# Query projection of a macaron block as a Strassen group, and first sums of weight pairs made by early adding transfers

## The chip, the cores and the metric

The kernel runs on one core of a Trainium2 chip. The metric is the device time of one execution in microseconds (us). The kernel before was timed three times. The engines are named as in the profile: PE (TensorE, matmuls), PEld (its weight loads), DVE (VectorE), ACT (ScalarE), POOL (GpSimd) and SP (SyncE); SP, ACT and POOL also issue transfers (DMAs).

## The reference

One encoder block on 256 frames of width 2048, in float32:

```python
x = x + 0.5 * swiglu_ffn(rmsnorm(x, g1), w_gate1, w_up1, w_down1)      # width 5632
h = rmsnorm(x, gm)
q_a, k_a, v_a, q_r, k_r, v_r, g_r, gate_a, gate_r = split(h @ w_in)    # 7 x 1024, 2 x 2048 columns
branch_a = chunked_band_attention(q_a, k_a, v_a, rel_bias) @ w_out_att # 8 heads of 128
branch_r = (silu(g_r) * retention(rotary(q_r), rotary(k_r), v_r)) @ w_out_ret
x = x + (sigmoid(gate_a) * branch_a + sigmoid(gate_r) * branch_r) @ w_out
x = x + 0.5 * swiglu_ffn(rmsnorm(x, g2), w_gate2, w_up2, w_down2)
return rmsnorm(x, gf)
```

Nearly all the work is matrix products of 256 rows with weights that are read once from HBM.

## The kernel before, in words

**Products in three parts.** Operands are split into a high part of reduced precision and the rest: ACT casts the high half (L129, tile hi), DVE subtracts it (L130, tile lo). A product takes three matmuls (L140, L141, L143): activation high with weight high, activation low with weight high, activation high with weight low. Matmuls run with 128x128 stationary activations and 512 weight columns.

**Plain steps.** A `Gemm` is a weight block of 512 columns; its K dimension is walked in steps of 256 rows. One step needs one weight transfer of 512 KB (raw, on SP's queue, five buffers), one split (one ACT and one DVE operation of 128x1024) and 2 x 2 x 3 = 12 matmuls. A job with K = 2048 has 8 steps.

**Strassen groups.** Two weight blocks of 512 columns that multiply the same activations are taken together as a 2x2 block product (rows halves by K halves) with 7 instead of 8 block products. A group has 28 steps of 6 matmuls: three phases of 8 (four r steps and four s steps, one for each of four pairs jc of row slices) and a last phase of four s steps. For each pair, two weight tiles k and x (512 KB each) come by POOL's queue (L543). The first sum x + k is formed either by DVE (`first`, L532) when the pair's r step is prepared, or by a transfer that adds in place (L547) for the pairs in `added`. In the second phase DVE adds a loaded weight to x (L594) and forms x - k (L580), and POOL issues a further adding transfer (L581). POOL's queue is strictly in order. The FFNs pass `ADDED`; the mixers' groups passed nothing, so there DVE formed all four first sums.

**Order.** All steps of the program stand in one list. `weave` lays it out: `lead` plain steps first, then the groups, with plain steps put between pairs of group steps. After each pair, a credit grows by rate x share of that place (`SHARE`, `MIX_SHARE`); from 0.6 on (0.2 at the end of a phase), and always at the end of the third phase, one plain step follows. A down projection's step may come only when `at_hand` says that its input is ready. `run` walks the list: before step c, up to four later steps are prepared (splits); then functions that are due at c (`later`, `at`) are called; then its matmuls are issued. Each engine executes in this program order, so a late DVE operation delays all DVE operations behind it. Loads of groups are released by `room["kept"]`: 8 transfers ahead, and `extra` more where `weave` is told so (the FFNs).

**Stages.** First FFN (10 groups, block 10 plain: a gate job and an up job; then down jobs), mixers (7 plain jobs and 5 groups woven, `mixed` is the step after), one more plain job, the retention's query and key jobs with attention and retention between them, output projections, second FFN. In the first FFN the plain gate job starts before the norm's scale is known: its results wait in two banks of tag z until `GATE_WAIT` steps later Silu is applied (L748), while the squares for the norm are summed by ACT (L429) in steps 8 to 11, two per step. `att_qk_done`, `nat_done` scale a projection; `to_transposed` transposes it on PE. Attention heads start at `mixed` + 4, one every four steps; q, k and v stay in SBUF from their projection until then (the pool of act tiles has 30 buffers).

Of the kernel before, what the change touches and what calls it, by code (L numbers as in the profile page):

```python
# [8 lines left out]
F32 = mybir.dt.float32  # L9
# [6 lines left out]
P = 128  # L16
# [24 lines left out]
MIX_LEAD = 8  # L41
RET_WAIT = (14, 5)
HELD = 6

MIX_SHARE = (0.85,) * 4 + (1.0,) * 4 + (0.8,) + (0.4,) * 3 + (0.15,) * 4
SHARE = (0.75,) * 4 + (1.0,) * 4 + (0.0,) * 4 + (0.2,) * 4
ADDED = (2, 3)
PLAIN = 10
PASSES = ((10,),) + tuple((b,) for b in range(10))
GATE_WAIT = 5  # L50
WARM = (6, 3)
TAIL_PARTS = ((0, slice(0, NB)), (1, slice(0, NB // 2)), (1, slice(NB // 2, NB)))

# [22 lines left out]
def block_kernel(ctx: ExitStack, tc: tile.TileContext, x, g1, w1g, w1u, w1d, gm, w_in, rel, woa, wor, wo,  # L76
# [439 lines left out]
    class Strassen:  # L516
# [2 lines left out]


        def __init__(self, norm, w1, col1, w2, col2, evict, added=()):
            self.added = added
# [15 lines left out]
        def loads(self):  # L538


            def go(tiles, i, jc):
                tiles[jc] = apool.tile([P, KC, NB], F32, tag="act", name=f"{self.name}{'kx'[i]}{jc}")
                nc.gpsimd.dma_start(tiles[jc], chunk(self.w[i], self.rows(0, jc), self.col[i]))  # L543

            def add_on():
                for jc in self.added:
                    nc.gpsimd.dma_start(self.x[jc], chunk(self.w[0], self.rows(0, jc), self.col[0]), accum_op=ALU.add)  # L547

            out = [
                lambda tiles=tiles, i=i, jc=jc: go(tiles, i, jc)  # L550
                for jc in range(HALF_K // KC) for i, tiles in enumerate((self.kept, self.x))
            ]
            out[-1] = lambda last=out[-1]: [last(), add_on()]
            return out

        def steps(self):

# [9 lines left out]
        def step(self, phase, jc, of_sum):  # L567
            made = {}
            name = f"{self.name}{phase}{jc}{'rs'[of_sum]}"
            n = HALF_K // KC  # L570

            def load():
                made["raw"] = weights_tile(f"raw{name}")
                i = 2 - phase
                fetch(made["raw"], self.w[i], self.rows(1, jc), self.col[i])

            def third():

                x, k = self.x[jc], self.kept[jc]
                nc.vector.tensor_sub(k, x, k)  # L580
                nc.gpsimd.dma_start(x, chunk(self.w[0], self.rows(1, jc), self.col[0]), accum_op=ALU.add)  # L581

            def prep():
                x = self.x[jc]
                if not of_sum:
                    if phase == 0:
                        made["w"] = split(self.kept[jc], name)
                        if jc not in self.added:
                            self.first(jc)
                        return  # L590
# [12 lines left out]

            bank, form, fresh, closing = {
# [4 lines left out]
            }[phase, of_sum]  # L609

            def products():
                hi, lo = made["w"]
                if fresh and jc == 0:
                    self.bank(bank)
                three([
                    (
                        self.acc[bank], self.norm.form(form, KC * jc + i), (hi[:, i, :], lo[:, i, :]),
                        fresh and jc == 0 and i == 0, closing and jc == n - 1 and i == KC - 1,
                    )
                    for i in range(KC)  # L620
                ], True)
# [59 lines left out]
    def weave(jobs, apart, groups, lead, share, start=None, extra=0):  # L681
# [5 lines left out]
        def next_standard():  # L687

            if len(queue) <= apart:
                return False  # L690
            job, k = queue[0]
            if any(at_hand.get(b, len(steps) + 1) > len(steps) for b in job.needs):
                return False
            steps.append(standard(job, k))
            del queue[0]
            if job.makes is not None and k + KC == job.nk:
                at_hand[job.makes] = len(steps) + 6
            return True

        for _ in range(lead):  # L700
# [27 lines left out]
    def ffn(name, norm, wg, wu, wd, after, start=None):  # L728
# [10 lines left out]
        def plain(b):  # L739
            gates = {}  # L740

            wait = GATE_WAIT if start is not None and b == PLAIN else 0

            def gate_done(acc):
                def go():
                    for t in range(NT):
                        gates[t] = tmp_tile(f"{name}g{b}{t}", "gate", 2)
                        nc.scalar.activation(gates[t], acc[t], AF.Silu, scale=norm.scale(t))  # L748

                if wait:  # L750
                    later(wait, go)
                else:
                    go()

            def up_done(acc):
                for t in range(NT):
                    a = gates[t]
                    nc.vector.scalar_tensor_tensor(a, acc[t], norm.scale(t), a, op0=ALU.mult, op1=ALU.mult)  # L758
                later(4, lambda: put_mid(b, gates))

            tags = ("acc", "acc")
            up = Gemm(wu, 0, b * NB, D // P, norm, up_done, tags)
            up.makes = b
            return [Gemm(wg, 0, b * NB, D // P, norm, gate_done, ("z", "z") if wait else tags), up]

        def paired(b):
            got = {}
# [59 lines left out]
    QA, KA, VA, QR, KR, VR, GR, GA, GG = 0, W, 2 * W, 3 * W, 4 * W, 5 * W, 6 * W, 7 * W, 7 * W + D  # L827
    scale = HD ** -0.5
    tposed, nat = {}, {}

    def heads_t(ts):
        return slice(ts * P, (ts + 1) * P)

    def to_transposed(key, b, srcs, steps):

        dst = act_tile(F32, f"{key}{b}T")
        tposed[key, b] = dst

        def go(t):
            ps = transpose4(srcs[t], f"{key}{b}p{t}").rearrange("p (i q) -> p i q", i=4)  # L840
# [4 lines left out]

        for t in range(NT):
            later(steps[t], lambda t=t: go(t))

    def att_qk_done(key, b):
        def done(acc):  # L850
# [40 lines left out]
    def nat_done(key, b, func, after=None):  # L891
        def done(acc):
            dst = act_tile(F32, f"{key}{b}")
            nat[key, b] = dst.rearrange("p a q -> p (a q)").rearrange("p (t n) -> p t n", t=NT)
            for t in range(NT):
                nc.scalar.activation(nat[key, b][:, t, :], acc[t], func, scale=nm.scale(t))
            if after is not None:
                after()

        return done  # L900
# [63 lines left out]
    def all_attention():  # L964
        for h in range(HEADS):
            for s, stage in attention(h):
                later(2 + 4 * h + s, stage)

    def retention(b):

# [65 lines left out]
    def gates(col1, col2, func, dsts):  # L1036
# [235 lines left out]
```

## Time and profile before

| | |
|---|---|
| median of three runs | 2061.91 us (2061.66 to 2061.99) |
| the profiled execution, its time | 2061.97 us |
| its span in the profile | 2060.1 us |
| PE, DVE, ACT, POOL busy | 2037.8, 1766.2, 1494.1, 344.8 us |
| matmuls | 9208 |
| moved by transfers | 498.47 MB, mean 242 GB/s |
| granted TensorE clock | 0.998 |

All durations below come from the one profiled execution. Its time and its span differ by 1.9 us of start and end around the program. A line of the costliest groups or of the timeline names line, engine, operation, out<-in by the program's tile names (buffer numbers left out); in the timeline, start and duration stand first, and in brackets the engine's idle time before it with what ended it. A group's tiles are named by the step at which the group stands: in z118, hiz11801s is the high half of phase 0, pair 1, s step. In rows of stages: start:end length, then busy us and instructions for PE, PEld, DVE, ACT, POOL; granted clock; share of the 16 DMA engines; GB/s.

### The profile page before, as it was taken

The page shows a single profiled execution, that of the slowest core. Times are in us where ns is not written, and L with a number is a line of the kernel's source. Part 1 is how long each engine was busy: PE and PEld are TensorE (multiplying, and loading weights), DVE is VectorE, ACT ScalarE, POOL GpSimd, SP SyncE. Part 2 cuts the span into 40 slices and gives each one's busy share as a digit, 9 for nine tenths or more (in the row PEclk, how much of TensorE's full clock was granted, in tenths as well). Part 3 has the DMA queues.
Part 4 walks back from the last instruction along what each step waited for, and adds up shares of the span by engine and source line. Part 5 has one row for each costly group of instructions (what it writes and reads, how often), then busy time and mean ns, then how long its engine had stood idle before and what let it go on. Part 6 is the DMA issues. An engine that isn't in the chain of part 4 may idle for free.

```text
span 2060.1 us, 26318 instructions
## 1 busy us (share of the span) xinstructions
PE 2037.8 (99%) x9208; PEld 1685.6 (82%) x9208; DVE 1766.2 (86%) x1836; ACT 1494.1 (73%) x1892; POOL 344.8 (17%) x386
## 2 busy tenths in 40 slices
PE   9999999999999999999999999999999999999998
PEld 7888888888888888888888888888888888888886
DVE  7999999999999799889966667569989999989996
ACT  8778877887877767776765434556788888887875
POOL 2221222221222110121100000012122212112200
PEclk9999999999999999999999999999999999999999
DMA  9888899888888677898786645578889888889983
GB/s 308 252 232 260 252 274 273 254 229 252 254 250 244 241 206 262 263 288 240 228 277 184 216 142 189 185 231 218 267 267 278 255 255 234 269 261 268 276 214 133
DMA packets 230325, 498.47 MB, mean 242 GB/s; under 512 B 15584, under 2 KB 16336, under 8 KB 230192
## 3 DMA queue, kind: packets, MB, share of 16 engines
q1 hardware_dynamic: 156736, 301.50, 43.5%
q0 software_dynamic: 70112, 189.44, 36.0%
q10 hardware_dynamic: 3344, 5.84, 0.8%
q8 instruction: 72, 1.18, 0.2%
q14 instruction: 61, 0.50, 0.1%
HBM read 487.81 MB, written 8.91 MB: 241 GB/s over the span
## 4 chain that ended last, share of the span: by engine, by line
PE 92%; ACT 3%; DVE 3%; issue 1%; DMA 1%; DVEq 0%; ACTq 0%; POOLq 0%; POOL 0%
PE acc L143 15%; PE acc L140 15%; PE acc L141 15%; DVE lo L130 1%; DMA raw<-in_w_in_dram 1%; ACT hi L129 0%; PE z392a L143 0%; PE z873a L140 0%; PE z910a L141 0%; PE z765a L141 0%; PE z543a L143 0%; PE z430a L143 0%; PE z801a L143 0%; PE z392a L141 0%; PE z505a L143 0%
## 5 line engine op out<-in xcount | busy, mean ns | idle before, releaser
L130 DVE TENSOR_TENSOR lo<-raw,hi 128x1024 fp32r<-128x1024 f32 x367 | 447.1, 1221 | 142.6 <-ACT hi L129 140.8
L129 ACT CAST hi<-raw 128x1024 fp32r<-128x1024 f32 x367 | 384.3, 1051 | 173.3 <-PE acc L141 138.0
L794 ACT ACTIVATE xall<-acc 128x512 f32<-128x512 f32 x160 | 94.5, 591 | 14.5 <-PE acc L143 10.3
L791 ACT ACTIVATE acc<-xall 128x512 f32<-128x512 f32 x160 | 95.8, 599 | 8.2 <-DVE f1g L758 4.3
L140 PE MATMUL acc<-hi,mgh 128*128 128x512 f32 x128 | 50.2, 392 | 0.0
L141 PE MATMUL acc<-hi,mgl 128*128 128x512 f32 x128 | 49.8, 389 | 0.0
L140 PE MATMUL acc<-hi,nma01h 128*128 128x512 f32 x96 | 38.8, 404 | 0.1
L140 PE MATMUL acc<-hi,nma00h 128*128 128x512 f32 x96 | 38.6, 402 | 0.0
L141 PE MATMUL acc<-hi,nma00l 128*128 128x512 f32 x96 | 37.5, 390 | 0.0
L141 PE MATMUL acc<-hi,nma01l 128*128 128x512 f32 x96 | 37.5, 390 | 0.0
L140 PE MATMUL acc<-hi,nma10h 128*128 128x512 f32 x96 | 37.5, 390 | 0.0
L141 PE MATMUL acc<-hi,nma11l 128*128 128x512 f32 x96 | 37.4, 390 | 0.0
L140 PE MATMUL acc<-hi,nma11h 128*128 128x512 f32 x96 | 37.4, 390 | 0.0
L141 PE MATMUL acc<-hi,nma10l 128*128 128x512 f32 x96 | 37.4, 390 | 0.0
L143 PE MATMUL acc<-lo,mgh 128*128 128x512 f32 x128 | 35.5, 389 | 0.0
L143 PE MATMUL acc<-lo,nma01h 128*128 128x512 f32 x96 | 29.6, 390 | 0.0
L143 PE MATMUL acc<-lo,nma11h 128*128 128x512 f32 x96 | 29.6, 389 | 0.0
L143 PE MATMUL acc<-lo,nma00h 128*128 128x512 f32 x96 | 29.6, 389 | 0.0
L143 PE MATMUL acc<-lo,nma10h 128*128 128x512 f32 x96 | 29.6, 389 | 0.0
L143 PEld LDWEIGHTS acc<-lo,mgh 128*128 128x128 f32 x128 | 24.0, 188 | 5.0
L141 PEld LDWEIGHTS acc<-hi,mgl 128*128 128x128 f32 x128 | 24.0, 188 | 4.9
L140 PEld LDWEIGHTS acc<-hi,mgh 128*128 128x128 f32 x128 | 24.0, 188 | 4.8
(6634 smaller groups left out, 7134.3 us busy)
## 6 DMA issues: line engine op xcount, KB each, us to landing
raw<-in_ffn_w_down_dram SPq DMA_DIRECT2D x176, 512.0 KB, 7.6
raw<-in_w_in_dram SPq DMA_DIRECT2D x96, 512.0 KB, 4.7
raw<-in_w_out_dram SPq DMA_DIRECT2D x32, 512.0 KB, 4.1
raw<-in_ffn_w_up_dram SPq DMA_DIRECT2D x16, 512.0 KB, 6.4
raw<-in_w_out_att_dram SPq DMA_DIRECT2D x16, 512.0 KB, 4.3
raw<-in_w_out_ret_dram SPq DMA_DIRECT2D x16, 512.0 KB, 3.9
raw<-in_ffn_w_gate_dram SPq DMA_DIRECT2D x15, 512.0 KB, 4.8
z392x<-in_w_in_dram POOLq DMA_DIRECT2D x8, 512.0 KB, 7.5
```

What stands on the lines that cost most here:

```text
L129: nc.scalar.copy(hi, raw)
L130: nc.vector.tensor_sub(lo, raw, hi.bitcast(F32))
L140: nc.tensor.matmul(acc, ahi, whi, start=first, stop=False, **more)
L141: nc.tensor.matmul(acc, alo, whi, start=False, stop=False, **more)
L143: nc.tensor.matmul(acc, ahi, wlo, start=False, stop=last, **more)
L791: nc.scalar.activation(acc, xs[t][:, cols], AF.Copy, scale=2.0)
L794: nc.scalar.activation(xs[t][:, cols], acc, AF.Copy, scale=0.5)
```

## The change

- The two query jobs (`QA`) become a sixth group of the mixers, `queries`, the first in order. Its results are scaled and transposed as the jobs' were. The second half of the retention's values (`VR`) moves from behind the weave into it. The weave then has 6 plain jobs and 6 groups, where it had 7 and 5; `MIX_SHARE` is changed.
- The mixers' groups get `ADDED` and the two extra loads (`EXTRA`).
- `ADDED` is (0, 1) instead of (2, 3), and the adding transfer is issued `ADD_WAIT` = 6 steps after the pair's x load, not behind the last load. If the pair's r step is prepared before that, DVE makes the sum and no transfer is issued.
- Transposed queries and keys and the attention's values are written to DRAM from ACT's queue and read back on POOL's queue (`put_away`, `bring_back`).
- In the first FFN, the plain gate's results go to banks of tag acc, are copied out by ACT at once, and Silu is applied in place 16 steps later; the squares come in steps 8 to 15, one per step.
- Down projections are held back 9 instead of 6 steps after the plain up job. Attention starts at `mixed` + 3, with heads 3 and 4 steps apart in turn (`HEAD_AT`).

```diff
-MIX_SHARE = (0.85,) * 4 + (1.0,) * 4 + (0.8,) + (0.4,) * 3 + (0.15,) * 4
+HEAD_AT = (3, 6, 10, 13, 17, 20, 24, 27)
+MIX_SHARE = (0.5,) * 4 + (1.0,) * 4 + (0.0,) * 4 + (0.2,) * 4
-ADDED = (2, 3)
+ADDED = (0, 1)
+ADD_WAIT = 6
-GATE_WAIT = 5
+GATE_WAIT = 16
+SQUARES = 8
...
-            def add_on():
-                for jc in self.added:
+            def add_on(jc):
+                if jc not in self.summed:
+                    self.summed.add(jc)
                     nc.gpsimd.dma_start(self.x[jc], chunk(self.w[0], self.rows(0, jc), self.col[0]), accum_op=ALU.add)
...
+            def second(jc):
+                go(self.x, 1, jc)
+                if jc in self.added:
+                    later(ADD_WAIT, lambda: add_on(jc))
...
-                        if jc not in self.added:
+                        if jc not in self.summed:
+                            self.summed.add(jc)
                             self.first(jc)
...
-                at_hand[job.makes] = len(steps) + 6
+                at_hand[job.makes] = len(steps) + 9
...
             def gate_done(acc):
-                def go():
+                for t in range(NT):
+                    gates[t] = tmp_tile(f"{name}g{b}{t}", *(("qk", 4) if wait else ("gate", 2)))
+
+                def go(srcs):
                     for t in range(NT):
-                        gates[t] = tmp_tile(f"{name}g{b}{t}", "gate", 2)
-                        nc.scalar.activation(gates[t], acc[t], AF.Silu, scale=norm.scale(t))
+                        nc.scalar.activation(gates[t], srcs[t], AF.Silu, scale=norm.scale(t))
                 if wait:
-                    later(wait, go)
+                    for t in range(NT):
+                        nc.scalar.copy(gates[t], acc[t])
+                    later(wait, lambda: go(gates))
                 else:
-                    go()
+                    go(acc)
...
-            return [Gemm(wg, 0, b * NB, D // P, norm, gate_done, ("z", "z") if wait else tags), up]
+            return [Gemm(wg, 0, b * NB, D // P, norm, gate_done, tags), up]
...
+    def put_away(table, key, b, tile):
+        nc.scalar.dma_start(to_dram[key][b], tile)
+        del table[key, b]
+
+    def bring_back(b):
+        for table, key in ((tposed, "qa"), (tposed, "ka"), (nat, "va")):
+            t = act_tile(F32, f"{key}{b}back")
+            nc.gpsimd.dma_start(t, to_dram[key][b])
+            table[key, b] = t if table is tposed else by_tokens(t)
...
-                later(2 + 4 * h + s, stage)
+                later(HEAD_AT[h] + s, stage)
...
-        return Strassen(nm, w_in0, col1, w_in0, col2, evict)
+        return Strassen(nm, w_in0, col1, w_in0, col2, evict, ADDED)
...
+    def queries():
+        srcs = [{}, {}]
+
+        def evict(t, side, r):
+            if side == 0:
+                bank, r = r, tmp_tile(f"qa0{t}", "gate", 2)
+                nc.scalar.activation(r, bank, AF.Copy, scale=nm.scale(t))
+            srcs[side][t] = r
+            if len(srcs[side]) == NT:
+                to_transposed("qa", side, srcs[side], (3, 3))
+
+        return Strassen(nm, w_in0, QA, w_in0, QA + NB, evict, ADDED)
+
+    groups = {"qa": queries, **groups}
     weave(
-        [proj(QA + b * NB, att_qk_done("qa", b), both) for b in range(2)]
-        + [proj(KA + b * NB, att_qk_done("ka", b), both) for b in range(2)]
+        [proj(KA + b * NB, att_qk_done("ka", b), both) for b in range(2)]
         + [proj(VA + b * NB, nat_done("va", b, AF.Copy), both) for b in range(2)]
-        + [proj(VR, nat_done("vr", 0, AF.Copy), both)],
-        0, groups, MIX_LEAD, MIX_SHARE,
+        + [proj(VR + b * NB, nat_done("vr", b, AF.Copy), both) for b in range(2)],
+        0, groups, MIX_LEAD, MIX_SHARE, None, EXTRA,
     )
     mixed = len(steps)
-    add([proj(VR + NB, nat_done("vr", 1, AF.Copy))])
...
-    for b in range(D // NB):
-        at(D // NB * 2 + b, lambda b=b: [n1.square(b, t) for t in range(NT)])
+    for i in range(NT * D // NB):
+        at(SQUARES + i, lambda i=i: n1.square(i // NT, i % NT))
...
-    at(mixed + 2, all_attention)
+    at(mixed - 3, lambda: bring_back(0))
+    at(mixed + 5, lambda: bring_back(1))
+    at(mixed, all_attention)
```

More of the change, by code (lines that the diff above doesn't have):

```diff
@@ L521, in __init__ @@
         def __init__(self, norm, w1, col1, w2, col2, evict, added=()):
-            self.added = added
+            self.added, self.summed = added, set()
             self.norm, self.w, self.col, self.evict = norm, (w1, w2), (col1, col2), evict
@@ L543, in go @@
                 nc.gpsimd.dma_start(tiles[jc], chunk(self.w[i], self.rows(0, jc), self.col[i]))
-            def add_on():
-                for jc in self.added:
+            def add_on(jc):
+                if jc not in self.summed:
+                    self.summed.add(jc)
                     nc.gpsimd.dma_start(self.x[jc], chunk(self.w[0], self.rows(0, jc), self.col[0]), accum_op=ALU.add)
-            out = [
-                lambda tiles=tiles, i=i, jc=jc: go(tiles, i, jc)
-                for jc in range(HALF_K // KC) for i, tiles in enumerate((self.kept, self.x))
-            ]
-            out[-1] = lambda last=out[-1]: [last(), add_on()]
-            return out
+            def second(jc):
+                go(self.x, 1, jc)
+                if jc in self.added:
+                    later(ADD_WAIT, lambda: add_on(jc))
+            return [
+                (lambda jc=jc: second(jc)) if i else (lambda jc=jc: go(self.kept, 0, jc))
+                for jc in range(HALF_K // KC) for i in range(2)
+            ]
         def steps(self):
@@ L829, in block_kernel, with by_tokens @@
     tposed, nat = {}, {}
+    to_dram = {key: [dram.tile([P, 4, SEQ], F32, name=f"{key}{b}d") for b in range(HEADS // 4)] for key in ("qa", "ka", "va")}
+    def put_away(table, key, b, tile):
[6 more added lines that the diff above has]
+            table[key, b] = t if table is tposed else by_tokens(t)
+    def by_tokens(t):
+        return t.rearrange("p a q -> p (a q)").rearrange("p (t n) -> p t n", t=NT)
     def heads_t(ts):
@@ L837, in to_transposed @@
         tposed[key, b] = dst
+        home = to_dram.get(key)
         def go(t):
@@ L847, in to_transposed @@
             later(steps[t], lambda t=t: go(t))
+        if home is not None:
+            later(max(steps) + 1, lambda: put_away(tposed, key, b, dst))
     def att_qk_done(key, b):
@@ L893, in done @@
             dst = act_tile(F32, f"{key}{b}")
-            nat[key, b] = dst.rearrange("p a q -> p (a q)").rearrange("p (t n) -> p t n", t=NT)
+            nat[key, b] = by_tokens(dst)
             for t in range(NT):
                 nc.scalar.activation(nat[key, b][:, t, :], acc[t], func, scale=nm.scale(t))
+            if key in to_dram:
+                put_away(nat, key, b, dst)
             if after is not None:
```

## The prediction

> **What bounds the kernel now.** I read the page first (busy time, chain), then the waits of PE, then the timeline where PE waits, then sums by stage.
>
> ```profile
> PE 2037.8 (99%) x9208; PEld 1685.6 (82%) x9208; DVE 1766.2 (86%) x1836; ACT 1494.1 (73%) x1892; POOL 344.8 (17%) x386
> PE 92%; ACT 3%; DVE 3%; issue 1%; DMA 1%; DVEq 0%; ACTq 0%; POOLq 0%; POOL 0%
> ```
>
> PE is busy 99% of the span and holds 92% of the chain: the number of matmuls sets the time, and beside it only the few waits of PE. How long is one matmul? A busy row lasts 0.39 us because matmuls overlap, so I take starts:
>
> ```profile
> 161.36 0.39 PE L140 MATMUL z46a<-hiz4630s,n1a11h 128*128 128x512 f32 x1
> 165.44 0.39 PE L140 MATMUL z46a<-hiz4633s,n1a11h 128*128 128x512 f32 x1
> ```
>
> Between them lie three group steps of 6 matmuls: 4.08 / 18 = 0.2267 us each. PE's waits, in total, times, longest:
>
> ```profile
> PE acc L143 <- DVE lo L130: 4.9, 9, 0.6
> PE z10c L140 <- ACT f1g L748: 2.2, 1, 2.2
> PE acc L141 <- DVE f2a10l L380: 1.4, 1, 1.4
> PE z1018c L143 <- DVE loz101800s L130: 0.6, 1, 0.6
> PE z982c L143 <- DVE loz98200s L130: 0.5, 1, 0.5
> PE acc L141 <- DVE f1a10l L380: 0.5, 1, 0.5
> ```
>
> These, about 10 us, are what an edit of order can win; matmuls taken away come on top.
>
> **Part 1, queries as a group: -5.4 us.** Two query jobs are 16 plain steps of 12 matmuls, 192; a group is 28 steps of 6, 168. PE loses 24 x 0.2267 = 5.4 us, all of it on the path. What hides the rest of the group is DVE, ACT and the transfers, priced in parts 5 and 6.
>
> **Part 2, first FFN, group starts: -5.5 us.** PE waits nine times for a plain step's low half; one case:
>
> ```profile
> 231.86 0.40 PE L141 MATMUL acc<-hi,f1a1l 128*128 128x512 f32 x1
> 232.78 0.73 PE L143 MATMUL acc<-lo,f1a1h 128*128 128x512 f32 x2 [0.53 <-DVE lo L130]
> 226.97 1.22 DVE L130 TENSOR_TENSOR loz11800r<-z118k,hiz11800r 128x1024 fp32r<-128x1024 f32 x1
> 228.11 1.22 DVE L532 TENSOR_TENSOR z118x<-z118x,z118k 128x1024 f32<-128x1024 f32 x1
> 230.38 1.22 DVE L532 TENSOR_TENSOR z118x<-z118x,z118k 128x1024 f32<-128x1024 f32 x1
> 231.51 1.22 DVE L130 TENSOR_TENSOR lo<-raw,hi 128x1024 fp32r<-128x1024 f32 x1
> ```
>
> The start comes 0.92 - 0.23 = 0.69 us late. DVE is in one run, an operation each 228.11 - 226.97 = 1.14 us, and two of them ahead of the late one are first sums of pairs 0 and 1 (L532). With ADDED = (0, 1) transfers make these, and DVE's sums of pairs 2 and 3 come behind the late operation: it is ready 2.28 us earlier, against 0.69 wanted. The next release to come last is the low half of the following steps, which keeps the same DVE total one or two plain steps later, where each plain step gives PE 12 x 0.2267 = 2.7 us for 1.14 of DVE. Eight of the nine go (the first, behind group z10, is in part 4): 8 x 0.69 = 5.5. Bounds: 0 (the wait moves to the later sums) to 6.2.
>
> The new wait is POOL's: the early sum of pair 1 may be issued only when that pair's load has landed.
>
> ```profile
> 226.11 1.24 POOL L547 DMA_DIRECT2D z118x<-in_ffn_w_up_dram  x1 [11.61 <-DMA z118x<-in_ffn_w_gate_dram]
> 230.36 1.22 POOL L547 DMA_DIRECT2D z118x<-in_ffn_w_up_dram  x1 [3.01 <-DMA z118x<-in_ffn_w_gate_dram]
> 231.70 1.05 ACT L129 CAST hiz11801s<-z118x 128x1024 fp32r<-128x1024 f32 x1 [0.19 <-DVE z118x L532]
> 238.34 0.39 PE L140 MATMUL z118c<-hiz11801s,n1s5h 128*128 128x512 f32 x1
> ```
>
> Now the adds of pairs 2 and 3 wait for their loads at 226.1 and 230.4, 4.25 us for two loads each; pair 1's load is two further ahead, landed by about 222. But its add is queued behind pair 3's load, so its data come after 230.4, at about 233: the cast of 231.70 starts some 1.5 us late, of 238.34 - 232.75 = 5.6 us in hand. Behind the waiting add on POOL stand only loads of the group after next and, 20 us on, the adds of L581. Cost 0; if two more microseconds were lost everywhere it would still be 0.
>
> **Part 3, second FFN: -1.5 us.** The same sums stand ahead of the waits of z982c and z1018c: 0.5 + 0.6 of idle, and 0.16 each from idle to start as above, -1.4. The wait for f2a10l:
>
> ```profile
> 1459.50 0.39 PE L140 MATMUL acc<-hi,f2a10h 128*128 128x512 f32 x1
> 1461.28 0.50 PE L141 MATMUL acc<-hi,f2a10l 128*128 128x512 f32 x1 [1.39 <-DVE f2a10l L380]
> ```
>
> 1.78 - 0.23 = 1.55 us. at_hand + 9 holds the first plain step back by three more, so that wait goes, but three pairs of steps then follow without a plain step between them, DVE being the slower there; I give back half, net -0.8. In the first group of this FFN the adds fall due after the pairs are prepared, so all four sums are DVE's, two more than now (2.28 us); a third of that, +0.7, reaches PE. Bounds of part 3: -3.0 to +0.8.
>
> **Part 4, the start: -1 us.** GATE_WAIT 16 and the squares from step 8 remove the largest wait:
>
> ```profile
> 44.50 0.61 PE L143 MATMUL acc<-lo,n1a11h 128*128 128x512 f32 x2
> 47.31 0.50 PE L140 MATMUL z10c<-hiz1000s,n1s5h 128*128 128x512 f32 x1 [2.19 <-ACT f1g L748]
> 49.66 0.63 PE L140 MATMUL z10a<-hiz1002r,n1a00h 128*128 128x512 f32 x1
> 50.51 0.63 PE L140 MATMUL z10a<-hiz1002r,n1a00h 128*128 128x512 f32 x1
> ```
>
> 47.31 - 44.95 = 2.4 us, and then a slow clock: 49.66 to 50.51 is 0.425 a matmul; eight starts take 3.20 instead of 1.81, 1.4 more. The Trainium skill ("TensorE: Matmul & The Clock Gate", What's actually happening) halves the clock after an idle window of some 3.4 us; here 2.19 us were enough, so the trace differs, and by the Trainium skill's figure the removed wait would be worth 1.4 us less.
>
> The gate's banks are now copied out and reused: up's second bank waits for the first copy, with half a step, 6 x 0.2267 = 1.4 us, in hand against a copy of half the size of the 1.05 us cast above: 0, at worst some tenths. But PE does not keep the 3.8 us, since DVE is next:
>
> ```profile
> 30.00:60.00 30.00, 27.80 (x116) 22.49 (x115) 27.05 (x34) 25.38 (x42) 3.19 (x3) 0.94 0.76 233
> 60.00:84.00 24.00, 24.00 (x112) 19.98 (x111) 23.02 (x23) 13.76 (x15) 7.02 (x8) 1.00 0.88 228
> 84.00:109.00 25.00, 24.46 (x107) 19.48 (x106) 22.89 (x23) 21.71 (x28) 6.79 (x10) 1.00 1.02 334
> 83.48 1.23 DVE L130 TENSOR_TENSOR loz1021r<-rawz1021r,hiz1021r 128x1024 fp32r<-128x1024 f32 x1 [0.98 <-ACT hiz1021r L129]
> 84.85 0.65 PE L143 MATMUL z10b<-loz1021r,n1a01h 128*128 128x512 f32 x2
> ```
>
> From 30 to 84 DVE is idle for 3.9 us in all, and at its end loz1021r is done at 84.71, PE uses it at 84.85: 0.14 us to spare, with the stall included. This first group too loses its two adds to DVE (+2.28). So of 3.8 us at most the idle less the new work, 3.9 - 2.3 = 1.6, can be kept up to this point; of the waits at f1a10l (0.5) and the first of the nine (0.69) perhaps some. I take -1.0; bounds -5.0 (all of it) to +2.
>
> **Part 5, first group of the mixers: +2.2 us.** MIX_SHARE puts two plain steps into its first phase where three stood, and none between the steps of its third phase where two stood. Slack now, at the end of the first phase:
>
> ```profile
> 740.10 1.22 DVE L130 TENSOR_TENSOR loz39203s<-z392x,hiz39203s 128x1024 fp32r<-128x1024 f32 x1
> 742.33 0.61 PE L143 MATMUL z392c<-loz39203s,nms5h 128*128 128x512 f32 x2
> ```
>
> 742.33 - 741.32 = 1.0 us. Each plain step taken away costs 2.7 - 1.14 = 1.6 us of slack, and the four sums stay with DVE here (the adds are due too late, as before there were none). One step less: 0.6 short; two more later: I add 1.6. Bounds 0 to 4.
>
> **Part 6, the rest of the mixers and the attention: +1.5 us.**
>
> ```profile
> 166.80:228.42 61.62, 61.08 (x273) 50.30 (x272) 56.55 (x53) 49.24 (x61) 13.23 (x14) 1.00 0.87 254
> 705.50:1050.50 345.00, 344.74 (x1539) 285.64 (x1540) 311.76 (x291) 243.52 (x273) 55.71 (x63) 1.00 0.80 251
> 1582.69:1643.43 60.74, 60.74 (x274) 50.38 (x272) 56.61 (x53) 49.34 (x61) 13.21 (x14) 1.00 0.89 261
> q1 hardware_dynamic: 156736, 301.50, 43.5%
> q0 software_dynamic: 70112, 189.44, 36.0%
> ```
>
> The first and third rows are one FFN group each, the second the mixers' woven steps. DVE there: 196 splits become 216, 20 first sums 14, other sums 40 become 48, so 22 x 1.14 + 1.4 = 26 us more, 338 us. PE: (6 x 168 + 48 x 12) x 0.2267 = 359.1, and the 2.2 us by which 345.0 exceeds today's 1512 x 0.2267: 361.3. DVE's share becomes 0.935, that of the third row (0.932), where PE never waits. ACT: 20 casts more on 243.5. Transfers of 0.524 MB: q1 has 575 in 896 us, 1.56 each; q0 361 in 742 us, of which 140 add by the code, so, the others at 1.56, an add takes 2.83. Mixers now: 0.80 x 345.0 = 276; a group brings 16 x 1.56 + 4 x 2.83 = 36.3, early adds 10 x 2.83 = 28.3, putting q, k, v away 9.4, eight weights fewer -12.5: 337.5, a share of 0.93 against 0.87 to 0.89 in an FFN group. I allow 1.5 us for late transfers and for attention heads that start 3.5 instead of 4 steps apart; bounds 0 to 6.
>
> Sum: -5.4 - 5.5 - 1.5 - 1.0 + 2.2 + 1.5 = -9.7. The profiled execution took 2061.97 us for a span of 2060.1, the median is 2061.91: 2052.2.
>
> **Rivals.** (a) The start keeps all it wins and the mixers cost nothing: -5.4 - 5.5 - 1.4 - 1.55 - 5.0 = -18.9, 2043. For it: ACT, 25.4 of 30 busy around the stall, is relieved. Against: 0.14 us of slack at 84.7. (b) The sums do not leave the burst but move it, or the adds come so late that DVE makes them after all: parts 2 and 3 are 0, part 4 is 0: -5.4 + 3.7 = -1.7, 2060. For it: the add is behind three loads. Against: the slack of 5.6 us. (c) The mixers become bound by transfers, slower than before. If the share that they can hold is what the FFN groups show, 0.88, the woven steps take 337.5 / 0.88 = 383.5, 22.2 more than by PE: 2052.2 + 22.2 - 1.5 = 2073. It decides from where the excess passes 11.2 us, at a share below 337.5 / 372.5 = 0.906. For it: the adds. Against: 84.00:109.00 holds 1.02, and PE waits for no weight in the FFN groups. The Trainium skill says that all queues share the same 16 engines ("Trainium Kernel Development and Optimization", Key Constraints), which speaks against added transfers; its limit of some 358 GB/s for a core's HBM ("DMA: Bandwidth & Descriptors", Specifications) speaks for the change: by an estimate, 251 GB/s x 345.0 us plus 28 transfers are 101 MB, in 361 us 280 GB/s. The rows decide by share: 228 GB/s stood at 0.88.
>
> **How the numbers follow.** Forecast 0.62, (a) 0.14, (b) 0.16, (c) 0.08. The forecast's own bounds are 2045 to 2059.5; that range with part of (a) and (b) beyond it leaves out some 2 in 10. A measurement of this kernel can tell about 0.2%, 4.1 us, from no change: forecast and (a) are faster, (b) the same, (c) slower.
>
> **What would show it.** Right: 24 fewer matmuls of 512 columns; the nine waits of acc for lo down to one or none; no 2.2 us wait of z10c, but short waits for DVE in z10 from 60 us on, group z46 starting only some 1 us before 105; short waits for lo in the mixers' first group; a transfer share there of 0.9 to 0.95. Wrong: z46 starting 4 us or more earlier (a), waits at steps 5 to 8 of every group (b), waits of PE's casts for raw or z..x transfers all through the mixers (c).

## The result and the profile after

| | before | after |
|---|---|---|
| median of the runs compared | 2061.78 us (2061.62 to 2061.99) | 2074.11 us (2072.80 to 2076.55) |
| ratio, 95% interval | | 1.0064 [1.0052, 1.0076] |
| the profiled execution, its time and span | 2061.97, 2060.1 us | 2073.62, 2071.7 us |
| matmuls | 9208 | 9184 |
| moved by transfers | 498.47 MB | 510.00 MB |

Slower by 12.3 us, where 9.7 us less were forecast. "Before" and "after" stand for the two kernels from here on. The page of after, busy time, two queues and chain:

```profile
PE 2042.8 (99%) x9184; PEld 1680.5 (81%) x9184; DVE 1785.4 (86%) x1856; ACT 1497.1 (72%) x1908; POOL 363.9 (18%) x410
q1 hardware_dynamic: 154560, 297.31, 42.6%
q0 software_dynamic: 74848, 202.03, 38.3%
PE 86%; DMA 5%; DVE 3%; issue 3%; ACT 2%; POOL 1%; ACTq 0%; DVEq 0%; POOLq 0%
```

The 24 matmuls are gone, yet PE is busy 5 us longer, and its share of the chain falls from 92% to 86% while DMA's rises from 1% to 5%. The waits of PE in after (total, times, longest):

```profile
PE z740c L143 <- ACT hiz74000s L132: 3.3, 1, 3.3
PE z427c L143 <- ACT hiz42700s L132: 3.0, 1, 3.0
PE acc L146 <- DVE lo L133: 1.6, 3, 0.6
PE z10c L146 <- DVE loz1003s L133: 1.3, 1, 1.3
PE z496c L143 <- ACT hiz49601s L132: 0.9, 1, 0.9
PE z10b L146 <- DVE loz1023r L133: 0.9, 1, 0.9
PE z462c L143 <- ACT hiz46201s L132: 0.6, 1, 0.6
```

Of the forecast's signs the 24 matmuls fewer are there, the nine waits of acc for lo became three, none of them in a group of the FFNs behind z10, and the 2.2 us wait of z10c for f1g is gone. New are two waits of 3 us, each in the second group of its weave: z427 follows z392, the first group of the mixers; z740 follows z704, the first of the second FFN. Where the 11.7 us of span arose, by the first matmul of a group in each trace:

| stretch | before | after | difference | forecast |
|---|---|---|---|---|
| to the first matmul of z46 | 105.20 | 108.46 | +3.3 | -1.0 |
| z46 to the mixers' first group z392 | 620.34 | 612.87 | -7.5 | -5.5 |
| z392 to the second FFN's first group | 670.51 | 682.38 | +11.9 | -1.7 |
| from there to the end of the span | 664.03 | 668.04 | +4.0 | -1.5 |

(1.25 us of the first row arose before z10, 0.8 of it in PE's wait for the gains, 1.8 instead of 1.0 us. It is not a cost of the change: in the first experiment below, with the same start, z10 begins at 39.55 us, as in before, and not at 40.76.) The wait of z427, on the queue of POOL, in ACT and in PE (start, duration; idle before it and what ended it in brackets):

```profile
762.74 1.17 POOL L546 DMA_DIRECT2D z427x<-in_w_in_dram  x1
763.46 1.17 POOL L546 DMA_DIRECT2D z427k<-in_w_in_dram  x1
764.18 1.17 POOL L546 DMA_DIRECT2D z427x<-in_w_in_dram  x1
773.87 1.23 POOL L551 DMA_DIRECT2D z427x<-in_w_in_dram  x1 [8.53 <-DMA z427x<-in_w_in_dram]
```

```profile
777.57 1.06 ACT L132 CAST hiz42701r<-z427k 128x1024 fp32r<-128x1024 f32 x1 [0.30 <-PE z392a L144]
786.19 1.04 ACT L132 CAST hiz42700s<-z427x 128x1024 fp32r<-128x1024 f32 x1 [7.56 <-DMA z427x<-in_w_in_dram]
```

```profile
787.28 0.79 PE L143 MATMUL z427c<-hiz42700s,nms5h 128*128 128x512 f32 x1 [2.97 <-ACT hiz42700s L132]
787.87 0.63 PE L144 MATMUL z427c<-hiz42700s,nms5l 128*128 128x512 f32 x1
788.30 0.63 PE L143 MATMUL z427c<-hiz42700s,nms5h 128*128 128x512 f32 x1
788.73 0.63 PE L144 MATMUL z427c<-hiz42700s,nms5l 128*128 128x512 f32 x1
```

L551 is the early add of pair 0. POOL can issue it only when x0 has landed (772.89), and by then the four loads k1, x1, k2, x2 stand in the queue (issued 762.0 to 764.2; by the trace they land one after the other from 776.0 to 782.2). The add's data come behind them, 12.2 us after its issue, at 786.09. The cast of that sum waits for it, and as ACT runs in program order the casts behind it wait too: ACT is idle for 7.6 us and PE for 3.0. Then come some matmuls 0.43 us apart instead of 0.2267, at a granted clock of 0.50 from 786.80 to 790.20. From the third group on k0 and x0 come as the two extra loads, half a group ahead, and nothing more is queued until the add: in z462 it was issued at 794.30 and landed 6.0 us later. But the add of pair 1 always has the loads of pairs 2 and 3 ahead: 13.2 to 13.4 us in z462, z496 and z531. In the mixers, where fewer plain steps lie in between, that is too late by a little each time:

```profile
852.39 1.05 ACT L132 CAST hiz46201s<-z462x 128x1024 fp32r<-128x1024 f32 x1 [4.17 <-DMA z462x<-in_w_in_dram]
911.81 1.04 ACT L132 CAST hiz49601s<-z496x 128x1024 fp32r<-128x1024 f32 x1 [4.85 <-DMA z496x<-in_w_in_dram]
```

### The profile page after: what moved, and what is told of

Read it like the earlier page. It is cut to its first block, busy times and chain, and to the rows that moved or that the text cites. A ratio compares the mean times of both kernels' runs of the same rounds, so it can differ in the third digit from the quotient of the medians.

```text
span 2071.7 us, 26346 instructions
## 1 busy us (share of the span) xinstructions
PE 2042.8 (99%) x9184; PEld 1680.5 (81%) x9184; DVE 1785.4 (86%) x1856; ACT 1497.1 (72%) x1908; POOL 363.9 (18%) x410
## 4 chain that ended last, share of the span: by engine, by line
PE 86%; DMA 5%; DVE 3%; issue 3%; ACT 2%; POOL 1%; ACTq 0%; DVEq 0%; POOLq 0%
PE acc L146 14%; PE acc L143 14%; PE acc L144 14%; DMA z531x<-in_w_in_dram 1%; DMA z462x<-in_w_in_dram 1%; DMA raw<-in_w_in_dram 1%; DMA z496x<-in_w_in_dram 1%; DMA z427x<-in_w_in_dram 1%; DMA z740x<-in_ffn_w_up_dram 1%; DVE lo L133 0%; ACT hi L132 0%; PE z922a L143 0%; PE z885a L144 0%; PE z262a L143 0%; PE z118a L143 0%
## 5 line engine op out<-in xcount | busy, mean ns | idle before, releaser
L133 DVE TENSOR_TENSOR lo<-raw,hi 128x1024 fp32r<-128x1024 f32 x351 | 426.5, 1219 | 118.1 <-ACT hi L132 116.5
L132 ACT CAST hi<-raw 128x1024 fp32r<-128x1024 f32 x351 | 366.9, 1050 | 151.4 <-PE acc L144 124.0
L143 PE MATMUL acc<-hi,nma01h 128*128 128x512 f32 x80 | 32.5, 406 | 0.0
L143 PE MATMUL acc<-hi,nma00h 128*128 128x512 f32 x80 | 32.4, 404 | 0.0
L144 PE MATMUL acc<-hi,nma01l 128*128 128x512 f32 x80 | 31.3, 391 | 0.0
L144 PE MATMUL acc<-hi,nma00l 128*128 128x512 f32 x80 | 31.3, 391 | 0.0
L143 PE MATMUL acc<-hi,nma11h 128*128 128x512 f32 x80 | 31.2, 390 | 0.0
L143 PE MATMUL acc<-hi,nma10h 128*128 128x512 f32 x80 | 31.2, 390 | 0.0
L144 PE MATMUL acc<-hi,nma10l 128*128 128x512 f32 x80 | 31.2, 390 | 0.0
L143 PE MATMUL acc<-hi,atth 128*128 128x512 f32 x64 | 26.2, 410 | 0.0
## 6 DMA issues: line engine op xcount, KB each, us to landing
z427x<-in_w_in_dram POOLq DMA_DIRECT2D x10, 512.0 KB, 11.9
```

Of the source, the lines that this page charges most:

```text
L132: nc.scalar.copy(hi, raw)
L133: nc.vector.tensor_sub(lo, raw, hi.bitcast(F32))
L143: nc.tensor.matmul(acc, ahi, whi, start=first, stop=False, **more)
L144: nc.tensor.matmul(acc, alo, whi, start=False, stop=False, **more)
```

## The experiments

Theory Q: the early adds stand in the queue behind loads, and it is their place that costs. Rival T: the added transfers are too many for the 16 DMA engines, wherever they stand. For the start, theory D: DVE's operations set its pace. Before, timed again beside the experiments in three sets, had medians of 2061.27, 2061.47 and 2061.69 us; ratios are to the set that was timed together with the run. Stages, each from one profiled execution, in the rows of the table above:

| run | to z46 | first FFN | mixers, attention | second FFN |
|---|---|---|---|---|
| without adds in second groups | 107.33 | 612.48 | 675.35 | 665.03 |
| early adds in the FFNs only | 105.32 | 614.14 | 670.10 | 666.40 |
| start only | 104.65 | 620.30 | 670.33 | 663.60 |
| start, two sums left out | 104.18 | 619.46 | 670.07 | 663.60 |
| sixth group only | 105.02 | 620.34 | 670.00 | 664.12 |
| sixth group and extra loads | 105.13 | 620.28 | 670.24 | 664.28 |
| FFN adds from third group, start | 104.49 | 612.49 | 670.06 | 662.77 |
| the same with the sixth group | 104.17 | 612.78 | 670.17 | 664.80 |
| the same with pair 0's adds in the mixers | 105.04 | 612.50 | 669.04 | 663.51 |
| sixth group, no first sums in the mixers | 104.63 | 612.78 | 665.88 | 663.36 |
| mixers of before, no first sums there | 104.79 | 612.77 | 670.06 | 662.69 |
| FFN adds from third group, no start | 105.18 | 613.35 | 670.31 | 664.48 |

**Second groups without early adds.** After, and in `weave`:

```diff
             group = make()
+            if n == 1:
+                group.added = ()
```

> The changed kernel, except that the second group of each weave has no early adding transfers: DVE makes all four first sums there. Theory Q (queue order: where a weave's loads are not yet two ahead, the early add of pair 0 stands behind six loads and the cast waits for it): the 3.0 us wait in the mixers' second group and the 3.3 us wait in the second FFN's second group go, with the 1.5 and 2.6 us of slow clock behind them, some 10 us, and DVE gives 1 us back in each: 2065 us. Theory T (the mixers and the start are bound by the amount of transfers, the two waits only show it): two adds fewer of 3 us each change little: 2071 to 2073 us.

Measured: 2063.14 us (2060.95 to 2065.26), 1.0007 [0.9998, 1.0017], 11.0 us below after. In ACT's timeline the cast of z427 now waits for DVE's sum alone, and of PE's waits those of z427c and z740c for ACT are gone; the longest that are left in the mixers and the start are:

```profile
778.29 1.05 ACT L132 CAST hiz42700s<-z427x 128x1024 fp32r<-128x1024 f32 x1 [1.14 <-DVE z427x L535]
```

```profile
PE z531c L143 <- ACT hiz53101s L132: 0.7, 1, 0.7
PE z10c L146 <- DVE loz1003s L133: 1.3, 1, 1.3
```

Groups z427 and z740 shorten from 65.96 to 60.37 and from 69.87 to 66.59 us, by 5.6 and 3.3 us, where the visible waits were 3.0 and 3.3. In z427 what follows the wait (casts in a row, slow matmuls) costs nearly as much again; in z740 DVE now makes all four sums, and that takes a part of the gain back. Q holds for the two long waits. In the mixers 4.8 us above before remain. No run issues the adds of the second groups earlier; that they would then cost little is argued from z46 alone, whose add is issued 10.9 us ahead of the group and whose length is 61.13 us with adds, 60.73 without.

**Early adds in the FFNs only.** Before, with ADDED = (0, 1), ADD_WAIT and the functions of the diff that belong to them; start and mixers as before.

> The kernel before with the early adding transfers of pairs 0 and 1 alone, in the FFNs (mixers, start and attention as before). Theory Q: the first FFN gains 0.9 us a group as in the changed kernel's trace (7 us), the second FFN's second group loses some 4 to 6 us, its last two groups gain 1.4: 2057 to 2060 us. Theory T: as before within 2 us, 2060 to 2064, since the adds are as many as before.

Measured: 2058.20 us, 0.9985 [0.9975, 0.9994]. The first FFN wins 6.2 us, a group taking 60.77 instead of 61.60, and the second FFN loses 2.4:

```profile
PE z728c L144 <- DVE loz72802s L131: 1.6, 1, 1.6
```

```profile
1461.22 1.05 ACT L130 CAST hiz72801s<-z728x 128x1024 fp32r<-128x1024 f32 x1 [4.05 <-DMA z728x<-in_ffn_w_up_dram]
```

Most of that is its second group again, 66.97 instead of 65.18 us. Here the add of pair 1, landed 14.7 us after its issue, holds ACT's cast for 4.05 us, the operations behind it come late on DVE, and PE waits for one of them. The time is as Q has it, by a smaller loss in that group (1.8 us, not 4 to 6) and a smaller gain in the first FFN than were expected.

**The start only.** Before, with GATE_WAIT = 16, the squares from step 8, the gate's copies and `at_hand` + 9.

> The kernel before with the start alone: gate results copied out to SBUF, Silu 16 steps later, squares from step 8 one per step, down projections 9 steps behind. Theory D (the first woven group is bound by DVE, so the 3.8 us won at the stall are lost in its later phases): 2060 to 2062 us, with new short waits of PE for lo between 55 and 95 us. Rival: the stall and its slow clock are simply gone and only the two sums that the early adds give back to DVE there undo it: 2057.5 to 2058.5 us.

Measured: 2059.82 us, 0.9994 [0.9985, 1.0003], not clear of no change. The wait is gone and phase 0 of z10 shortens from 23.13 to 19.04 us, but phase 1 grows from 19.04 to 20.72 and the last two together from 23.51 to 25.67, the matmuls being the same in all. So z46 starts only 0.55 us earlier, 0.3 of it because z10 did. In rows of stretches (length; PE, PEld, DVE, ACT, POOL busy; clock; DMA share; GB/s), the third of them phase 1, and of PE's waits:

```profile
30.00:60.00 30.00, 30.00 (x134) 24.83 (x133) 27.46 (x36) 26.06 (x44) 3.19 (x3) 1.00 0.75 228
60.00:84.00 24.00, 23.04 (x98) 16.71 (x97) 23.03 (x22) 14.43 (x18) 8.26 (x10) 1.00 0.90 231
58.26:78.98 20.72, 20.10 (x86) 15.36 (x85) 20.72 (x20) 12.76 (x14) 3.61 (x3) 1.00 0.85 239
```

```profile
PE z10b L144 <- DVE loz1023r L131: 0.8, 1, 0.8
```

From 30 to 60 us PE now has no idle; from 60 to 84 it runs 98 matmuls, where before ran 112, and DVE is busy 96% of the time, in phase 1 all of it. The wait of PE shown, for DVE's loz1023r, follows at 90.11.

**The start without two sums.** To see whether DVE's earlier load decides, the first sums of pairs 0 and 1 of z10 are left out, so its product lacks a term:

```diff
-                            self.first(jc)
+                            if self.name != "z10":
+                                self.first(jc)
```

> e5 (start alone) with the first sums of pairs 0 and 1 of the first FFN's first group left out, so that the product of those pairs lacks a term: two DVE operations of 1.14 us fewer between 30 and 60 us. Theory D (this group is bound by DVE): 2057.5 to 2058.3 us, the start 1.5 to 2.3 us shorter than in e5. Rival (transfers or ACT bind it): as e5, 2059.8.

Measured: 2059.78 us, 0.9991 [0.9982, 1.0000]:

```profile
30.00:60.00 30.00, 30.00 (x134) 24.84 (x133) 25.83 (x34) 26.29 (x44) 3.19 (x3) 1.00 0.77 231
60.00:84.00 24.00, 23.03 (x99) 17.20 (x99) 23.03 (x22) 14.43 (x17) 8.75 (x10) 1.00 0.90 234
```

```profile
PE z10b L144 <- DVE loz1023r L131: 0.9, 1, 0.9
```

DVE has 1.6 us less to do before 60 us and the wait behind stays; z10 is 0.44 us shorter, the median the same. D as stated falls. What fits is that DVE binds in phase 1 by that phase's own work: steps are prepared at most four ahead, so idle time of DVE earlier can hardly be used for it. That is argued from the rows; no run takes work out of phase 1. Two sums more than in the start alone, as in after, do cost: z10 lasts 67.71 instead of 65.43 us there, 2.3 us, with the wait of z10c for loz1003s.

**The sixth group only.** Before, with `queries`, the new weave, storing and reading back, and `HEAD_AT`; no early adds, no extra loads in the mixers.

> The kernel before with the mixers' change alone and no early adds there: queries as a sixth group, new MIX_SHARE, values of the retention in the weave, queries, keys and values put away in DRAM and brought back, attention from mixed + 3. DVE makes all first sums of the mixers. Theory Q: 24 matmuls fewer (-5.4 us), some 2 us lost in the first group for want of plain steps, 1 us in the attention: 2059 us. Theory DVE (338 us of DVE work plus 10 sums of 1.14 in 361 us, 0.97, is too near one): waits for lo in every group, 2064 to 2070 us.

Measured: 2061.47 us, 1.0001 [0.9992, 1.0010]. 24 matmuls fewer, worth 5.4 us, and nothing is won. Both expectations miss: it is more than 2059 us, and PE has two waits for lo in the woven mixers, 1.0 us in all, not one in every group.

**The same with extra loads.**

```diff
-        0, groups, MIX_LEAD, MIX_SHARE,
+        0, groups, MIX_LEAD, MIX_SHARE, None, EXTRA,
```

> e6 (sixth group alone) with the two extra loads in the mixers and still no early adds. It parts the early adds of the mixers' third to sixth group from the loads ahead: the changed kernel with second groups by DVE spent 5.3 us more in the mixers and attention than e6. If the adds cost it (they and what queues behind them on the 16 engines): as e6, 2061 to 2062. If the loads ahead collide with the weights' own: 2064 to 2066.

Measured: 2060.83 us, 1.0000 [0.9991, 1.0010]. The loads cost nothing, so the 5 us by which the mixers of the first experiment are longer come from the early adds of groups three to six.

**FFN adds from the third group on, with the start.** Before, with the start's part; early adds (0, 1) only from the third group of a weave, and in the first two the late adds (2, 3) behind the last load, as before:

```diff
             group = make()
+            group.early = n >= 2
+            if group.added and not group.early:
+                group.added = LATE
...
+            if not self.early:
+                out = [
+                    lambda tiles=tiles, i=i, jc=jc: go(tiles, i, jc)
+                    for jc in range(HALF_K // KC) for i, tiles in enumerate((self.kept, self.x))
+                ]
+                out[-1] = lambda last=out[-1]: [last()] + [add_on(jc) for jc in self.added]
+                return out
```

> The kernel before with the start of the change and its early adds in the FFNs, but early adds (pairs 0 and 1) only from the third group of an FFN on; the first two groups keep the late adds of pairs 2 and 3. Mixers and attention as before. Theory Q: the loss of e3 in the second FFN's second group (some 5 us by its trace) is gone and the first FFN's gain stays: 2061.3 - 7 - 1.4 - 1.5 = 2051 us. Theory T: no better than e3, 2057 us, since the number of transfers is the same.

Measured: 2051.62 us (2051.36 to 2052.26), 0.9954 [0.9939, 0.9969], faster than both kernels, and no other run that makes all sums is faster. Of PE's waits for lo of plain steps one is left, in z10:

```profile
PE z10b L146 <- DVE loz1023r L133: 0.8, 1, 0.8
PE z728a L146 <- DVE loz72802r L133: 0.7, 1, 0.7
PE acc L146 <- DVE lo L133: 0.6, 1, 0.6
```

**The same without the start.**

> Kernel before plus the early adds from an FFN's third group alone, start and mixers as before. If start and adds are worth their own sums (start alone -1.7 us, both -9.8), 2061.5 - 8.1 = 2053.4; if the start's gain depends on the adds (DVE relieved at the first groups), this run comes out at 2056 or above.

Measured: 2053.74 us, 0.9964 [0.9952, 0.9977], as the sum has it. The two add up; the adds are the larger part.

**The same with the sixth group.** The fastest kernel with the change's mixers, without early adds and extra loads there.

> As e8, and the mixers with the sixth group but without early adds and without the two extra loads there. Theory Q with the result of e6 (the sixth group alone gains nothing): the same as e8, 2051 us. If the 24 matmuls fewer pay once the FFNs are in order: 2047 us.

Measured: 2052.61 us (2051.38 to 2053.69), 0.9958 [0.9944, 0.9973]; mixers and attention 670.17 against 670.06 us. The sixth group again wins nothing.

**Pair 0's early add in the mixers.** To that kernel, with the extra loads:

```diff
-        return Strassen(nm, w_in0, col1, w_in0, col2, evict)
+        return Strassen(nm, w_in0, col1, w_in0, col2, evict, (0,))
...
-        return Strassen(nm, w_in0, QA, w_in0, QA + NB, evict)
+        return Strassen(nm, w_in0, QA, w_in0, QA + NB, evict, (0,))
...
-                group.added = LATE
+                group.added = LATE if group.added == ADDED else ()
```

> The kernel with all but the mixers' early adds (2052.6 us), to which the mixers' groups from the third on get the early add of pair 0 alone, with the two extra loads. Theory 'place in the ring' (the add of pair 1 is the one that lands 12 to 13 us late, that of pair 0 comes while the ring is short): no short waits of PE for ACT's high halves, one first sum less per group on DVE, 2052.6 or up to 1 us below it. Theory 'amount' (each 512 KB that is read and added on top of a transfer share of 0.9 costs the same wherever it stands): half of the 5 us that eight adds cost, 2055.

Measured: 2051.87 us (2051.52 to 2052.81), 0.9954 [0.9942, 0.9967]. Each of the four adds lands 5.8 to 6.3 us after its issue, and neither PE nor ACT waits for one. From the first matmul of the mixers' first group to that of their last, in after, in this run, in the run without these adds:

```profile
721.33:1024.87 303.54, 294.43 (x1281) 236.56 (x1280) 269.43 (x245) 208.15 (x230) 65.55 (x70) 0.99 0.91 271
```

```profile
717.54:1008.17 290.63, 289.00 (x1281) 236.60 (x1280) 274.65 (x250) 208.73 (x230) 58.04 (x64) 1.00 0.91 275
```

```profile
716.95:1008.38 291.43, 289.37 (x1281) 236.36 (x1280) 277.92 (x253) 207.68 (x228) 53.23 (x60) 1.00 0.85 264
```

The DMA share is 0.91 in the first two rows, which differ by 12.9 us, and half of the adds cost nothing at all. So T, a price for each add wherever it stands, falls, and Q holds: the adds that stood behind loads are those that cost. But a mean share hides bursts. From issue to landing of pair 1's add the rows of after are, in the mixers' z462 and in z118 of the first FFN:

```profile
839.10:852.29 13.19, 13.19 (x60) 10.89 (x59) 9.93 (x9) 7.17 (x8) 2.70 (x3) 1.00 1.06 359
223.49:235.07 11.58, 11.58 (x52) 9.57 (x51) 8.70 (x10) 8.95 (x12) 2.70 (x3) 1.00 1.06 347
```

At a share of 1.06 the 16 engines have no room while the loads ahead of the add are drained. This is so in the FFN too, where PE never waits for it: the burst costs something only where a first use falls into it. Whether the add would land earlier in a burst if it stood ahead of the loads was not tried.

**Why the sixth group wins nothing.** In the kernel with the sixth group (2052.61) and in the one with the mixers of before (2051.62) all first sums x + k of the mixers' groups are left out, so those products lack a term:

```diff
-                            self.first(jc)
+                            if self.norm.name != "nm":
+                                self.first(jc)
```

> The kernel with all but the mixers' early adds (2052.6 us); here the first sums x + k of all groups of the mixers are left out, so their products lack a term. DVE loses 24 operations of 1.22 us, about 27 us of work in the mixers, and nothing takes their place on the transfers. Theory 'DVE' (the 5.4 us of the 24 matmuls taken away are lost because DVE, at 335 of 350 us, has no room left): the gain comes out, 5 us below the kernel with the mixers as before that leaves out the same sums, and 2047 to 2048 in all. Theory 'layout' (the loss comes from the attention's new start, the retention's values in the weave and the queries' transposes): 2051 to 2053, level with that kernel within 1.5 us.

> The kernel with the mixers as before (2051.6 us) and the first sums x + k of the mixers' five groups left out, so their products lack a term: the partner of the run with the sixth group. PE waits in these mixers for 2 us in all, so both theories expect 2050 to 2051.6.

Measured: 2048.77 us (0.9939 [0.9927, 0.9952]) with the sixth group, 2052.09 us (0.9955 [0.9941, 0.9968]) with the mixers of before. The stage from z392 on takes 665.88 and 670.06 us: now the sixth group wins 4.2 of its 5.4 us there, 3.3 by the medians, less than the 5 expected; the medians are 0.8 and 0.5 us above their expectations. With DVE relieved (the row below, 90% busy; 95% in the run without early adds in the mixers) the gain comes out, so it was DVE that held it; with five groups the same relief is worth nothing.

```profile
717.41:1004.89 287.48, 286.86 (x1281) 237.23 (x1280) 258.77 (x234) 210.99 (x230) 53.17 (x60) 1.00 0.86 267
```

Of the last 1.2 us, 0.9 lie in the group z531, which takes 58.06 us for 57.1 us of matmuls and has one wait of 0.6 us for a plain step's lo. What causes it stays open.

## Why the prediction was wrong

**The cost 0 of POOL's new wait (part 2)** is the step that failed most. It read the slack in z118, a group in the middle of its weave, and there it was right: pair 1's add landed 4.75 us after the group's first matmul (235.07, 230.32 in after), where the 233 worked out stand 4.6 us after it (228.42 in before), and PE waits for no add from the third group of an FFN on. But every weave has a second group, for which no extra loads were let in. There the add of pair 0, the first sum that is needed, is the one behind four loads. How far ahead of its group it is issued decides: 10.9 us in z46 (97.56 against 108.46), which goes without a wait of PE; 7.5 us in z427 (773.87, 781.34) and 6.9 us in z740 (1457.64, 1464.49), which wait 3 us. Without the adds of the second groups after comes down by 11.0 us; by the traces 7.0 of it lie in the mixers and 3.0 in the second FFN. The trace of before has what was needed for this: when x0 lands in each second group, how long before the group begins, and which loads are issued in between.

**Part 6** carried z118's slack over to the mixers by way of a DMA share. There pair 1's adds of four groups cost 6.3 us (675.35 against 669.04): they land 5.0, 8.1 and 7.5 us after the first matmul of z462, z496 and z531. The 1.5 us allowed were for late transfers; the quantity that decides, 13 us from issue to landing against the time to first use, was not worked out for the mixers.

**Part 1** had the 24 matmuls right and their worth wrong: "DVE's share becomes 0.935, that of the third row (0.932), where PE never waits". In the mixers' groups it is 0.95 without early adds and 0.945 with pair 0's, and the share of a stage does not tell what each group loses. With the sixth group only, the first two groups take 60.0 and 60.4 us. Their 252 matmuls are 57.1 us of PE and their 16 transposes 1.8 (in before z392 has 288 matmuls, 65.3 us, and 16 transposes, and takes 67.09), so they lose 1.1 and 1.4; the third loses 0.8, the fourth nothing, the fifth 1.4. **Part 5** gave the first group +2.2, twice what it lost, and nothing to the others.

**Part 2's gain** has the right mechanism and is larger: 0.87 us in each of eight groups, 7.0 us in the run without the start, where 8 x 0.69 were counted. The ninth wait, in z46, goes with the start (first FFN 613.35, with the start 612.49). In z118 of after the low half (DVE, done at 232.95) is ready a microsecond before its use (PE, 233.95), as DVE now makes its sums behind it (235.79):

```profile
231.73 1.22 DVE L133 TENSOR_TENSOR lo<-raw,hi 128x1024 fp32r<-128x1024 f32 x1
235.79 1.22 DVE L535 TENSOR_TENSOR z118x<-z118x,z118k 128x1024 f32<-128x1024 f32 x1
```

```profile
233.95 0.62 PE L146 MATMUL acc<-lo,f1a1h 128*128 128x512 f32 x2
```

**Part 3** was -1.5 and is +4.0: z740's add is 3.0 to 3.3 of that, two more sums of the first two groups by DVE 1.8 (66.59 against 64.81 us for the second group). Where these are left as before, the second FFN takes 662.7 to 664.8 us in five profiled executions, from 1.3 less to 0.8 more than in before; the forecast without its +0.7 for the sums is 2.2 less.

**Part 4** was -1.0. The start alone wins 0.55 up to z46, and the two sums given to DVE cost 2.3. That DVE takes back most of what the stall's end wins was right; the failed step is "of 3.8 us at most the idle less the new work, 3.9 - 2.3 = 1.6, can be kept": it counts idle time from 30 to 84 us as one store, and in the run without two sums 1.6 us less of DVE's work before 60 us make z10 only 0.44 us shorter.

**Rivals.** (c) gave 2073, near the time that was measured, and its sign appeared, casts that wait for z..x transfers in the mixers. But that its number fits is luck. Its mechanism, a mean share of 0.88 above which the mixers grow longer, is not what happened: 7.3 us of the excess over before lie in the start and the second FFN, and the mixers' groups ran at 0.91 in 290.63 us, as fast as at 0.85. What is full are the bursts of loads (1.06), and only adds that are needed within them cost time. (b)'s "the add is behind three loads" was the right object, weighed at the wrong group. What failed is the choice of the place at which the slack was read.

## What to carry to other kernels

A transfer that adds onto a loaded tile costs its place in an in-order queue: work out its landing as the landing of everything issued before it, and compare that with the first use, in the first, second and last round of each loop, not in a steady one. Give such adds to the tiles whose load is last in the queue, or to rounds whose loads are already in, and let the engine make the others. Matmuls taken away are won only where the engines that feed them have room phase by phase. A stage's mean share does not tell: at a DVE share of 0.93 a group of the FFN runs without a wait of PE, and at 0.95 the mixers lost 4.2 of 5.4 us.

## What the runs showed of the hardware

An early adding transfer of 512 KB in after lands 5.9 to 9.1 us after its issue, half of them within 6.1 us, when nothing is ahead of it in POOL's queue, and 11.5 to 13.4 us when four loads of 512 KB are. Those four loads land some 2.1 us after one another. A wait of 3.0 us on PE is followed by matmuls 0.43 us apart (787.87, 788.30, 788.73) at a granted clock of 0.50, and so is the 3.3 us one of z740. The Trainium skill ("TensorE: Matmul & The Clock Gate", What's actually happening) has the clock fall after an idle window of some 3.4 us. Here waits of 2.97 and 3.28 us were enough, and 2.19 us in before.
